# Shift and scale of both streams in a one-layer hybrid trunk: eight weight units in one run of requests, and one unsplit product in four column parts of the array

## The chip, the cores and the metric

The kernel runs on one core of a Trainium2 chip. The metric is device time in microseconds (us) of one execution, on all-float32 data. Lower is better.

## What is computed

One layer of a trunk over a latent stream (256 tokens) and a context stream (256 tokens), 1024 wide. Cut to what the change touches:

```
silu_c, silu_cc = silu(c), silu(c_ctx)                      # one vector for each stream
sh1_l, sc1_l, g1_l, sh2_l, sc2_l, g2_l = split(silu_c @ w_ada + b_ada, 6)
sh1_c, sc1_c, ...                      = split(silu_cc @ w_ada + b_ada, 6)
pl = (xl * (1 + sc1_l) + sh1_l) @ w_in                      # latent
pc = (xc * (1 + sc1_c) + sh1_c) @ w_in                      # context
... four token mixers on pl, pc, output projection, norm ...
... 32 experts (top 4), w_gate, w_up, w_down: 1024 x 1024 each, norm ...
```

`w_ada` is 1024 x 6144. Its first two sections of 1024 columns (shift and scale, sections 0 and 1) are needed for both streams before the input projection can start. The other four are needed later and for the latent stream alone.

## The kernel before

**Stages.** A front (projections and token mixers, until about 370 us) and then a loop over 32 experts whose weights (402.7 MB in float32) stream through a ring of buffers. The front is six generators (`gdn`, `within`, `side`, `ada_late`, `prep`, `dense`) that a written string, `ORDER`, weaves step by step (`weave`): each letter runs one step of one generator. So every engine gets its instructions in a fixed order, and each engine works through its own in that order. SP issues nearly all loads (`load`, L266), also in a fixed order: a load whose buffer is not free holds up all loads behind it. The loads are counted on eight semaphores in turn, so a load also waits until the load eight places before it has landed.

**Weight units.** The weights of the front come in units of 1 MB (2 of the 8 row blocks of `w_ada` by 1024 columns), named by section and part: ada(0,0) to ada(0,3), ada(1,0) to ada(1,3). There are four buffers, "spots" (`ring` tags r0 to r3). `issue(spot)` asks for the next unit of that spot's queue and `done(key)` calls it when a unit has been read. Spots 0 to 3 first hold ada(0,h), then ada(1,h). Behind these, spots 0 and 1 take the projection weights `uB`, `uK`, `uV` and so on in turn, and spot 2 takes the later sections: ada(2,0) is its third unit. `beside` hangs other loads on a unit: the input `xT` in two halves behind ada(1,3) and behind the first half of `uB`.

**Shift and scale** (`ada_first`, L416 on, and `ada_tail`). For each unit two row blocks k are multiplied. The even one is split into a rounded part and a rest (ACT L434 and DVE L435, in buffer `adap`) and multiplied by the split vectors `s4` (4 columns: two streams, two parts) in four fast products of 512 columns (L438). The odd one is multiplied unsplit, as float32, in two products (L429). `ada_tail` copies the sums (4 rows) out of PSUM, turns them with 8 small transposes (L455) and adds the bias on DVE into `mod`.

**What follows.** `prep` makes the operands: for each k of product B it modulates the input (`modulate`, ACT L543, DVE L544 and L545) and splits the weight slice (`split`, ACT L552 and DVE L553). `dense` runs the products of B for each k: 12 matmuls of 432 columns (L557 to L559), then K, V and the rest. `ada_late` multiplies the units of the later sections by the vector on ACT (L643) and sums them on POOL (L645, L647). ACT's order has the first of these, on ada(2,0), between the operands of k = 2 and k = 3 of product B.

Of the kernel before, what the change touches and what calls it, by code (L numbers as in the profile page):

```python
# [11 lines left out]
F32 = mybir.dt.float32  # L12
# [11 lines left out]
D = 1024  # L24
# [174 lines left out]
def trunk(ctx: ExitStack, tc: tile.TileContext, I, out, offs, dbg=None, nexp=NE):  # L199
# [82 lines left out]
    pa, pb = (held.tile([128, 4096], F32, tag=f"pair{i}", name=f"before{i}") for i in range(2))  # L282
    va = pb[:, 0:width(oa)]
    load(va[:, 0:64], I['va'][:, 0:64])

    def A(k):
        o, n = oa[k]
# [30 lines left out]
    queues[0] += prods[0::2]  # L318
# [4 lines left out]
    def issue(spot):  # L323

        if not queues[spot]:
            return
        key = queues[spot].pop(0)
        u = ring.tile([128, 2048], F32, tag=f"r{spot}", name="u" + "_".join(str(x) for x in key))
        if key[0] == 'ada':
            _, sec, h = key  # L330
            u = u.rearrange("p (k f) -> p k f", k=2)
            load(u, w_ada[:, 2 * h:2 * h + 2, sec * D:(sec + 1) * D])
        elif key[0] == 'out':
            u = u.rearrange("p (k f) -> p k f", k=2)
            load(u, w_out[:, 2 * key[1]:2 * key[1] + 2])
        else:
            c, h = key
            width_ = sum(b - a for a, b in COLS[c])
            n = 8 if c in 'KV' else 4
            u = u[:, 0:n * width_].rearrange("p (k f) -> p k f", k=n)  # L340
            o = 0
            for a, b in COLS[c]:
                load(u[:, :, o:o + b - a], w_in[:, n * h:n * h + n, a:b])
                o += b - a
        for dst, src in beside.pop(key, []):
            load(dst, src)
        open_units[key], spot_of[key] = u, spot

    def take(key):
# [1 line left out]

    def done(key):

        issue(spot_of[key])

    for spot in range(4):
        issue(spot)


    places = {}  # L360
# [49 lines left out]
    s4 = cst.tile([128, 8, 4], F32R, name="s4")  # L410
    sT3 = sT.rearrange("p (k v) -> p k v", v=2)
    S_.activation(s4[:, :, 0:2], sT3, AF.Copy)
    V.tensor_sub(s4[:, :, 2:4], sT3, s4[:, :, 0:2])


    def ada_first():  # L416

        tails = []
        for sec in range(2):
            ps = [(bank, fbank)[sec](f"psada{sec}{n}") for n in range(2)]  # L420
            for h in range(4):
                if sec == 1:
                    next(tails[0], None)
                u = take(('ada', sec, h))
                for kk in range(2):
                    k = 2 * h + kk
                    if kk:
                        for n in range(2):
                            P_.matmul(ps[n][0:2], sT3[:, k], u[:, kk, n * 512:(n + 1) * 512], start=False, stop=(k == 7), skip_group_check=True)  # L429
                        done(('ada', sec, h))  # L430
                    else:
                        w2 = early([128, 2, D], F32R, (0, 1, 3)[(4 * sec + h) % 3], f"adap{sec}{k}")
                        hi, lo = w2[:, 0], w2[:, 1]
                        S_.activation(hi, u[:, kk], AF.Copy)  # L434
                        V.tensor_sub(lo, u[:, kk], hi)  # L435
                        for w in (hi, lo):
                            for n in range(2):
                                P_.matmul(ps[n][0:4], s4[:, k], w[:, n * 512:(n + 1) * 512], start=(k == 0 and w is hi), stop=False, skip_group_check=True)  # L438
                    yield
            tails.append(ada_tail(sec, ps))  # L440
        yield from tails.pop()
        have.add('mod')

    def ada_tail(sec, ps):

        r4 = fp.tile([128, D], F32, tag="kTn", name=f"r4{sec}")[0:4]
        for n in range(2):
            if sec and n:
                V.tensor_copy(r4[:, n * 512:(n + 1) * 512], ps[n][0:4])
            else:  # L450
                S_.activation(r4[:, n * 512:(n + 1) * 512], ps[n][0:4], AF.Copy)
# [5 lines left out]
        p4 = pt[:, 0:32].rearrange("p (c v) -> p c v", v=4)  # L457
        V.tensor_tensor(mod[:, sec], p4[:, :, 0:2], bada[:, 8 * sec:8 * sec + 8].unsqueeze(2).to_broadcast([128, 8, 2]), op=OP.add)
        V.tensor_tensor(mod[:, sec], mod[:, sec], p4[:, :, 2:4], op=OP.add)
        if sec == 1:  # L460
            V.tensor_single_scalar(mod[:, sec], mod[:, sec], 1.0, op=OP.add)

# [235 lines left out]
        V.scalar_tensor_tensor(dst, u, 3.0, less, op0=OP.subtract, op1=OP.mult)  # L698


    mst = early(list(I["masks"].shape), I32, 3, "mst")
    load(mst, I['masks'])
# [1402 lines left out]
```

## Time and profile before

| what | value |
|---|---|
| device time, three runs | 1442.87, 1443.89, 1446.61 us (median 1443.89) |
| profiled execution: its time, its span | 1443.94 us, 1442.0 us |
| PE / DVE / ACT / POOL busy | 80% / 34% / 21% / 13% of the span |
| bytes moved by DMA | 460.59 MB, mean 319 GB/s |
| section 0 and 1 of `w_ada`: first request, `mod` complete | 1.15 us, 46.6 us |
| first expert product | about 386 us |

The shares are averages over the front and the experts. The change lies in the first 60 us, so that stretch is to be read: when each load is asked for and lands, which engine waits for it, and what in that stretch the rest of the front hangs on.

### The profile page before, as it was taken

The page shows a single profiled execution, that of the slowest core. Times are in us where ns is not written, and L with a number is a line of the kernel's source. Part 1 is how long each engine was busy: PE and PEld are TensorE (multiplying, and loading weights), DVE is VectorE, ACT ScalarE, POOL GpSimd, SP SyncE. Part 2 cuts the span into 40 slices and gives each one's busy share as a digit, 9 for nine tenths or more (in the row PEclk, how much of TensorE's full clock was granted, in tenths as well). Part 3 has the DMA queues.
Part 4 walks back from the last instruction along what each step waited for, and adds up shares of the span by engine and source line. Part 5 has one row for each costly group of instructions (what it writes and reads, how often), then busy time and mean ns, then how long its engine had stood idle before and what let it go on. Part 6 is the DMA issues. An engine that isn't in the chain of part 4 may idle for free.

```text
span 1442.0 us, 26141 instructions
## 1 busy us (share of the span) xinstructions
PE 1150.8 (80%) x11226; PEld 708.8 (49%) x11226; DVE 489.6 (34%) x863; ACT 297.6 (21%) x576; POOL 192.5 (13%) x229
## 2 busy tenths in 40 slices
PE   6797999899697897787787988686677869767783
PEld 1576888678444544354333643353333434433342
DVE  3767767979511211212022211121121112211116
ACT  3456644444210111111010101010001001101012
POOL 0242243450200100010000100010000101000002
PEclk9998979999698998998797989898879989898997
DMA  7634334418796998999943999999999999999970
GB/s 286 239 110 131 111 117 148 175 67 317 317 419 262 417 420 357 418 416 417 385 159 129 412 419 418 417 418 416 419 412 419 408 408 420 405 417 418 416 287 30
DMA packets 129059, 460.59 MB, mean 319 GB/s; under 512 B 9488, under 2 KB 19088, under 8 KB 128048
## 3 DMA queue, kind: packets, MB, share of 16 engines
q1 hardware_dynamic: 128816, 457.52, 79.8%
q8 instruction: 131, 2.15, 0.6%
q14 instruction: 112, 0.92, 0.2%
HBM read 456.45 MB, written 1.05 MB: 317 GB/s over the span
## 4 chain that ended last, share of the span: by engine, by line
PE 54%; DMA 22%; DVE 11%; issue 8%; ACT 4%; SPq 1%; DVEq 0%; ACTq 0%
PE g L1768 18%; PE four L1768 11%; DMA ring<-in_w_down 11%; DMA ring<-in_w_up 6%; PE xb L1750 6%; PE four L1814 3%; DMA ring<-in_w_gate 2%; PE fb L1786 2%; DMA bd<-in_b_down 1%; DMA uada<-in_w_ada 1%; PE psada L429 1%; DVE gt L1794 1%; PE psW L1005 1%; ACT scr L1796 1%; SPq L266 1%
## 5 line engine op out<-in xcount | busy, mean ns | idle before, releaser
L1768 PE MATMUL g<-ring,X 128*32 128x256 f32 (+1 forms) x3680 | 355.9, 472 | 142.2 <-issue 87.5
L1768 PEld LDWEIGHTS g<-ring,X 128*32 128x32 f32 (+1 forms) x3680 | 157.2, 128 | 320.2 <-issue 233.8
L1768 PE MATMUL four<-ring,X 128*32 128x256 f32 (+1 forms) x2272 | 208.6, 435 | 20.3 <-DMA ring<-in_w_down 19.6
L1824 DVE SCALAR_TENSOR_TENSOR rows<-four,cw,rows 128x1024 f32<-128x1024 f32 x66 | 81.7, 1280 | 329.6 <-PE four L1814 329.6
L1794 DVE TENSOR_TENSOR gt<-fb,vc 128x256 f32<-128x256 f32 (+1 forms) x37 | 18.7, 504 | 423.7 <-PE fb L1786 423.7
L1768 PEld LDWEIGHTS four<-ring,X 128*32 128x32 f32 (+1 forms) x2272 | 86.0, 118 | 123.5 <-issue 60.9
L1750 PE MATMUL xb<-Sg,hl 128*128 128x96 f32 x1024 | 135.4, 288 | 4.5 <-DVE Sg L1736 2.6
L1750 PEld LDWEIGHTS xb<-Sg,hl 128*128 128x128 f32 x1024 | 125.6, 200 | 27.2 <-issue 24.6
L1736 POOL TENSOR_SCALAR Sq<-slots,rank 128x128 f32<-128x128 f32 x62 | 39.4, 647 | 580.8 <-PE xb L1758 342.2
L1772 ACT ACTIVATE sA<-g 128x256 f32<-128x256 f32 (+1 forms) x33 | 14.0, 423 | 342.5 <-PE g L1768 342.5
L645 POOL TENSOR_TENSOR adas<-adas,uada 128x1024 f32<-128x1024 f32 x24 | 59.8, 2492 | 99.3 <-ACT uada L643 98.9
L1736 POOL TENSOR_SCALAR Sg<-slots,rank 128x96 f32<-128x96 f32 x62 | 31.6, 521 | 301.1 <-PE xb L1750 257.3
L1752 ACT ACTIVATE X<-xb 128x384 f32<-128x384 f32 x64 | 31.4, 491 | 123.4 <-PE xb L1750 117.9
L1796 ACT ACTIVATE scr<-gt 128x256 f32<-128x256 f32 (+1 forms) x37 | 17.7, 480 | 172.8 <-DVE gt L1795 172.8
L1772 ACT ACTIVATE sA<-four 128x256 f32<-128x256 f32 (+1 forms) x30 | 12.8, 427 | 163.1 <-PE four L1768 163.1
L1814 PE MATMUL four<-sA,ST 32*128 32x256 f32 (+1 forms) x512 | 42.7, 406 | 1.6 <-DVE sA L1985 1.6
L643 ACT ACTIVATE uada<-uada,sT 128x1024 f32<-128x1024 f32 x32 | 35.7, 1140 | 9.4 <-DMA uada<-in_w_ada 9.2
L1802 DVE TENSOR_TENSOR X<-fb,vc 128x256 f32<-128x256 f32 (+1 forms) x36 | 18.0, 499 | 54.2 <-PE fb L1786 54.2
L1005 PEld LDWEIGHTS <-before 64*64 64x64 f16 x1088 | 29.8, 115 | 9.8 <-issue 3.8
L1814 PEld LDWEIGHTS four<-sA,ST 32*128 32x128 f32 (+1 forms) x512 | 28.1, 188 | 6.5 <-DVE sA L1985 2.1
L1797 DVE TENSOR_TENSOR gt<-gt,scr 128x256 f32<-128x256 f32 (+1 forms) x37 | 18.9, 510 | 20.5 <-ACT scr L1796 20.5
L1768 PE MATMUL four<-ring,Xm 128*64 128x512 f32 x96 | 21.1, 592 | 0.0
(560 smaller groups left out, 1558.0 us busy)
## 6 DMA issues: line engine op xcount, KB each, us to landing
ring<-in_w_gate SPq DMA_DIRECT2D x128, 1024.0 KB, 18.1
ring<-in_w_up SPq DMA_DIRECT2D x128, 1024.0 KB, 17.8
ring<-in_w_down SPq DMA_DIRECT2D x128, 1024.0 KB, 18.1
uada<-in_w_ada SPq DMA_DIRECT2D x24, 1024.0 KB, 5.3
uout<-in_w_out SPq DMA_DIRECT2D x4, 1024.0 KB, 5.2
uE<-in_w_in SPq DMA_DIRECT2D x2, 1024.0 KB, 5.5
uF<-in_w_in SPq DMA_DIRECT2D x4, 512.0 KB, 4.0
uG<-in_w_in SPq DMA_DIRECT2D x2, 1024.0 KB, 5.3
```

The costliest lines, as they stand in the source:

```text
L643: S_.activation(u[:, kk], u[:, kk], AF.Copy, scale=sT3[:, 2 * h + kk, 0:1])
L645: G_.tensor_tensor(acc_, acc_, u[:, kk], op=OP.add)
L1005: P_.matmul(ps[cs, x * 64:x * 64 + 64], L[cs, x], R[cs, x] if len(R.shape) == 3 else R[cs], start=True, stop=True, skip_group_check=True)
L1736: eng.tensor_scalar(Sm[:, t, 0:m * n].rearrange("p (q s) -> p q s", s=n), slots[:, a:a + n].unsqueeze(1).to_broadcast([128, m, n]), rank[: ...
L1750: P_.matmul(xb[:, o:o + n], hl[:, t, k * 128:(k + 1) * 128], Sm[:, t, 0:n], start=(k == ks[0] and t == 0), stop=(t == 1), skip_group_check ...
L1752: S_.activation(X[:, ks[0] * n:(ks[-1] + 1) * n], xb[:, 0:len(ks) * n], AF.Copy)
L1768: P_.matmul(ps[n * q:n * q + n, 0:m], x(k), w[:, kk * 1024 + q * m:kk * 1024 + (q + 1) * m], start=(k == 0), stop=(k == 7), skip_group_che ...
L1786: P_.transpose(fb[:, c * 128:(c + 1) * 128], s[:, c * 128:(c + 1) * 128], ident)
L1794: V.tensor_tensor(g, p, bias(Cv('bg'), e, n), op=OP.add)
L1796: S_.activation(sg, g, AF.Sigmoid, scale=1.702)
L1814: P_.matmul(four[:, b, t * 256:(t + 1) * 256], st_[n * q:n * q + n, t * 128:(t + 1) * 128], Y[n * q:n * q + n, i * 256:(i + 1) * 256], sta ...
L1824: V.scalar_tensor_tensor(a, ps[t], cw[:, t, e:e + 1], a, op0=OP.mult, op1=OP.add)
```

## The change

Three things change.

1. **Loads.** The four units of section 1 no longer wait for the spots of section 0. They get buffers of their own (`extra`: three ring buffers that the split had used or that are filled later, and the upper half of `pa`). SP asks for them right behind section 0, then for both halves of the input and the masks, and only then for anything that hangs on `done`. Spot 0 and 1 go on to `uB` and spot 2 to ada(2,0) as soon as the products of section 0 have read them.
2. **Products.** Nothing is split. The vectors stand in a zeroed array `s32` with 32 columns for each row block. Each unit takes four float32 products of 512 columns, one for each row block and column half, and each goes to its own 32 output rows (columns of the array): 32 products in all in place of 48.
3. **Tail.** One PSUM bank (128 rows) is copied out by ACT, turned in four 128 x 128 transposes, and DVE adds the bias and the two row-block parts with strided views.

```diff
+    extra = [early([128, 2048], F32, i, f"uada1{i}") for i in (0, 1, 3)] + [pa[:, 2048:4096]]
-    beside['ada', 1, 3] = [(xus[0], xT[0])]
-    beside['B', 0] = [(xus[1], xT[1])]
-    first_ada = [('ada', sec, h) for sec in range(2) for h in range(4)]
+    first_ada = [('ada', 0, h) for h in range(4)]
...
     for spot in range(4):
         issue(spot)
+    for h in range(4):
+        load(take(('ada', 1, h)), w_ada[:, 2 * h:2 * h + 2, D:2 * D])
+    mst = pb[:, 2048:2048 + I["masks"].shape[1]].bitcast(I32)
+    for dst, src in ((xus[0], xT[0]), (xus[1], xT[1]), (mst, I['masks'])):
+        load(dst, src)
...
+    s32 = pb[:, 3200:3456].rearrange("p (k v) -> p k v", v=32)
+    V.memset(s32, 0.0)
+    V.tensor_copy(s32[:, :, 0:2], sT3)
...
                 for kk in range(2):
-                    k = 2 * h + kk
-                    if kk:
-                        for n in range(2):
-                            P_.matmul(ps[n][0:2], sT3[:, k], u[:, kk, n * 512:(n + 1) * 512], start=False, stop=(k == 7), skip_group_check=True)
-                        done(('ada', sec, h))
-                    else:
-                        w2 = early([128, 2, D], F32R, (0, 1, 3)[(4 * sec + h) % 3], f"adap{sec}{k}")
-                        hi, lo = w2[:, 0], w2[:, 1]
-                        S_.activation(hi, u[:, kk], AF.Copy)
-                        V.tensor_sub(lo, u[:, kk], hi)
-                        for w in (hi, lo):
-                            for n in range(2):
-                                P_.matmul(ps[n][0:4], s4[:, k], w[:, n * 512:(n + 1) * 512], start=(k == 0 and w is hi), stop=False, skip_group_check=True)
-                    yield
+                    for n in range(2):
+                        q = 2 * kk + n
+                        P_.matmul(ps[32 * q:32 * q + 32], s32[:, 2 * h + kk], u[:, kk, n * 512:(n + 1) * 512], start=(h == 0), stop=(h == 3), skip_group_check=True)
+                done(('ada', sec, h))
+                yield
...
-        for c in range(8):
-            P_.transpose(pt[:, 4 * c:4 * c + 4], r4[:, c * 128:(c + 1) * 128], ident[0:4, 0:4])
+        for c in range(4):
+            P_.transpose(pt[:, 128 * c:128 * c + 128], r[:, c * 128:(c + 1) * 128], ident)
```

SP's order of loads (output tile, input, shape; in brackets what the issue waits for: a DMAHW is one of the eight semaphores of earlier loads, an engine's name is work of that engine), from the last unit of section 0 on. Before:

```order
L266 DMA cons_89<-in_cons 128x640
L266 DMA mst<-in_masks 128x1152
L266 DMA uada_0_150<-in_w_ada 128x2x1024 [waits DMAHW0_49,DMAHW1_49,DVE_49,PE_49]
L266 DMA uada_1_185<-in_w_ada 128x2x1024 [waits DMAHW3_49,DVE_49,PE_49]
L266 DMA uada_2_196<-in_w_ada 128x2x1024 [waits DMAHW2_49,DMAHW4_49,DVE_49,PE_49]
L266 DMA uada_3_207<-in_w_ada 128x2x1024 [waits DMAHW5_49,DVE_49,PE_49]
L266 DMA xu_92<-in_xT 128x2048
L266 DMA uB_224<-in_w_in 128x4x384 [waits DMAHW0_49,DVE_49,PE_49]
```

The same place after (`uada_87` to `uada_89` and the first `before_84` are section 1; `before_84` from `in_xT` is the second half of the input):

```order
L266 DMA cons_92<-in_cons 128x640
L266 DMA uada_87<-in_w_ada 128x2x1024
L266 DMA uada_88<-in_w_ada 128x2x1024 [waits DMAHW0_49]
L266 DMA uada_89<-in_w_ada 128x2x1024 [waits DMAHW1_49]
L266 DMA before_84<-in_w_ada 128x2x1024 [waits DMAHW2_49]
L266 DMA xu_95<-in_xT 128x2048 [waits DMAHW3_49]
L266 DMA before_84<-in_xT 128x2048 [waits DMAHW4_49]
L266 DMA before_85<-in_masks 128x1152 [waits DMAHW5_49]
L266 DMA uB_151<-in_w_in 128x4x384 [waits DMAHW6_49,PE_49]
```

Section 1 and the input now wait for earlier loads alone and no longer for DVE and PE; behind the masks the order of `uB`, `vb`, `cons` and ada(2,0) is as it was.

PE's order for section 1. Before, its second and third unit:

```order
L438 MATMUL psada_210<-adap_238,s_110 4x512 [waits Activation_49]
L438 MATMUL psada_211<-adap_238,s_110 4x512
L438 MATMUL psada_210<-adap_238,s_110 4x512 [waits DVE_49]
L438 MATMUL psada_211<-adap_238,s_110 4x512
L429 MATMUL psada_210<-uada_1_185,sT 2x512 [waits DMAHW1_49]
L429 MATMUL psada_211<-uada_1_185,sT 2x512
```

After, its second to fourth unit and the transposes of its tail:

```order
L438 MATMUL psada_199<-uada_88,before_85 32x512 [waits DMAHW0_49]
L438 MATMUL psada_199<-uada_88,before_85 32x512 x3
L438 MATMUL psada_199<-uada_89,before_85 32x512 [waits DMAHW1_49]
L438 MATMUL psada_199<-uada_89,before_85 32x512 x3
L438 MATMUL psada_199<-before_84,before_85 32x512 [waits DMAHW2_49]
L438 MATMUL psada_199<-before_84,before_85 32x512 x3
L452 MATMUL psadT_235<-cons_92,r_233 128x128 [waits DVE_49,Activation_49]
L452 MATMUL psadT_235<-cons_92,r_233 128x128 x3
```

PE now waits for the load of each unit alone; the waits for ACT and DVE inside a unit are gone, and everything behind the tail stands as before.

## Rows read from the trace of the kernel before

**Rows 1.** Page part 2: 40 equal slices, DMA busy tenths and GB/s
```profile
DMA  7634334418796998999943999999999999999970
GB/s 286 239 110 131 111 117 148 175 67 317 317 419 262 417 420 357 418 416 417 385 159 129 412 419 418 417 418 416 419 412 419 408 408 420 405 417 418 416 287 30
```

**Rows 2.** Chain that ended last, in time order: start us, us, what; 45 to 61
```profile
45.05 9.44 DMA uada<-in_w_ada
...
55.57 1.13 ACT uada L643
57.23 2.16 DVE xu L544
60.54 0.60 DVE hlB L553
```

**Rows 3.** Timeline of SP's issues: start us, us, engine line op out<-in xcount
```profile
14.75 16.04 SPq L266 DMA_DIRECT2D uada<-in_w_ada  x4
30.84 0.46 SPq L266 DMA_DIRECT2D xu<-in_xT  x1
...
45.05 14.58 SPq L266 DMA_DIRECT2D uada<-in_w_ada  x2
```

**Rows 4.** Timeline of ACT and PE, 46 to 59 us, idle before in brackets
```profile
46.61 0.60 ACT L543 ACTIVATE xl<-xu,mod 128x256 fp32r<-128x256 f32 x1 [2.07 <-DVE mod L461]
...
47.61 0.55 ACT L552 ACTIVATE hlB<-uB 128x432 fp32r<-128x432 f32 x1
...
54.51 2.19 ACT L643 ACTIVATE uada<-uada,sT 128x1024 f32<-128x1024 f32 x2 [3.48 <-DMA uada<-in_w_ada]
...
58.96 0.36 PE L557 MATMUL pB<-hlB,xl 128*128 128x432 f32 x1
```

**Rows 5.** DMA issues at 4.26, 30.84 and 45.05 us: KB, us to landing
```profile
cons<-in_cons SPq DMA_DIRECT2D x1, 320.0 KB, 12.1
...
xu<-in_xT SPq DMA_DIRECT2D x1, 1024.0 KB, 7.6
...
uada<-in_w_ada SPq DMA_DIRECT2D x1, 1024.0 KB, 9.4
```

**Rows 6.** Stretches: us, busy (instructions) by engine, PEclk, DMA share, GB/s
```profile
10.00:15.00 5.00, 5.00 (x9) 0.80 (x9) 3.35 (x7) 1.47 (x2) 0.00 (x0) 1.00 1.02 418
35.00:40.00 5.00, 5.00 (x22) 1.34 (x20) 3.46 (x9) 1.06 (x1) 0.00 (x0) 1.00 1.01 363
...
41.00:42.00 1.00, 1.00 (x4) 0.10 (x3) 0.29 (x1) 0.00 (x0) 0.00 (x0) 1.00 0.79 263
```

**Rows 7.** Timeline of PE and ACT: products, PSUM copy and transposes
```profile
21.13 3.57 PE L429 MATMUL psada<-uada,sT 128*2 128x512 f32 x4
25.69 1.88 PE L429 MATMUL psada<-uada,sT 128*2 128x512 f32 x4
...
29.57 0.59 ACT L451 ACTIVATE r<-psada 4x512 f32<-4x512 f32 x1 [7.65 <-PE psada L429]
...
230.42 0.63 PE L1017 MATMUL pskwT<-cons,kw 128*128 128x128 f32 x4 [0.98 <-DVE kw L1070]
...
398.47 3.66 PE L1768 MATMUL four<-ring,X 128*32 128x256 f32 x64
```

**Rows 8.** Product B at both clocks (timeline), and two stretches as in rows 6
```profile
50.01 0.56 PE L557 MATMUL pB<-hlB,xl 128*128 128x432 f32 x1
50.37 0.56 PE L558 MATMUL pB<-hlB,xl 128*128 128x432 f32 x1
...
58.76 0.36 PE L559 MATMUL pB<-hlB,xc 128*128 128x432 f32 x1
...
100.00:120.00 20.00, 19.22 (x169) 17.98 (x167) 17.18 (x37) 14.79 (x27) 4.79 (x2) 1.00 0.33 101
...
182.00:199.00 17.00, 17.00 (x164) 15.06 (x164) 7.67 (x14) 6.99 (x12) 4.39 (x2) 0.50 0.27 88
```

More of the change, by code (lines that the diff above doesn't have):

```diff
@@ L346, in issue @@
             load(dst, src)
+        if key[0:2] == ('ada', 0):
+            h = key[2]
+            open_units['ada', 1, h], spot_of['ada', 1, h] = extra[h].rearrange("p (k f) -> p k f", k=2), None
         open_units[key], spot_of[key] = u, spot
@@ L352, in done @@
     def done(key):
-        issue(spot_of[key])
+        if spot_of[key] is not None:
+            issue(spot_of[key])
     for spot in range(4):
         issue(spot)
+    for h in range(4):
[3 more added lines that the diff above has]
+        load(dst, src)
     places = {}
@@ L409, in trunk @@
     V.tensor_copy(bada, A('b_ada'))
-    s4 = cst.tile([128, 8, 4], F32R, name="s4")
     sT3 = sT.rearrange("p (k v) -> p k v", v=2)
-    S_.activation(s4[:, :, 0:2], sT3, AF.Copy)
-    V.tensor_sub(s4[:, :, 2:4], sT3, s4[:, :, 0:2])
+    s32 = pb[:, 3200:3456].rearrange("p (k v) -> p k v", v=32)
+    V.memset(s32, 0.0)
+    V.tensor_copy(s32[:, :, 0:2], sT3)
     def ada_first():
@@ L419, in ada_first @@
         for sec in range(2):
-            ps = [(bank, fbank)[sec](f"psada{sec}{n}") for n in range(2)]
+            ps = (bank, fbank)[sec](f"psada{sec}")
             for h in range(4):
@@ L424, in ada_first @@
                 u = take(('ada', sec, h))
+                yield
                 for kk in range(2):
-                    k = 2 * h + kk
-                    if kk:
-                        for n in range(2):
-                            P_.matmul(ps[n][0:2], sT3[:, k], u[:, kk, n * 512:(n + 1) * 512], start=False, stop=(k == 7), skip_group_check=True)
-                        done(('ada', sec, h))
-                    else:
-                        w2 = early([128, 2, D], F32R, (0, 1, 3)[(4 * sec + h) % 3], f"adap{sec}{k}")
-                        hi, lo = w2[:, 0], w2[:, 1]
-                        S_.activation(hi, u[:, kk], AF.Copy)
-                        V.tensor_sub(lo, u[:, kk], hi)
-                        for w in (hi, lo):
-                            for n in range(2):
-                                P_.matmul(ps[n][0:4], s4[:, k], w[:, n * 512:(n + 1) * 512], start=(k == 0 and w is hi), stop=False, skip_group_check=True)
-                    yield
+                    for n in range(2):
+                        q = 2 * kk + n
+                        P_.matmul(ps[32 * q:32 * q + 32], s32[:, 2 * h + kk], u[:, kk, n * 512:(n + 1) * 512], start=(h == 0), stop=(h == 3), skip_group_check=True)
+                done(('ada', sec, h))
+                yield
             tails.append(ada_tail(sec, ps))
@@ L444, in ada_tail @@
     def ada_tail(sec, ps):
[L446 to L451, printed above, removed]
+        r = t512(f"r{sec}")
+        S_.activation(r, ps, AF.Copy)
         yield
         pt = xbank(f"psadT{sec}")
-        for c in range(8):
-            P_.transpose(pt[:, 4 * c:4 * c + 4], r4[:, c * 128:(c + 1) * 128], ident[0:4, 0:4])
+        for c in range(4):
+            P_.transpose(pt[:, 128 * c:128 * c + 128], r[:, c * 128:(c + 1) * 128], ident)
         yield
-        p4 = pt[:, 0:32].rearrange("p (c v) -> p c v", v=4)
-        V.tensor_tensor(mod[:, sec], p4[:, :, 0:2], bada[:, 8 * sec:8 * sec + 8].unsqueeze(2).to_broadcast([128, 8, 2]), op=OP.add)
-        V.tensor_tensor(mod[:, sec], mod[:, sec], p4[:, :, 2:4], op=OP.add)
+        p4 = pt.rearrange("p (c k n v) -> p k n c v", c=4, k=2, n=2)[:, :, :, :, 0:2]
+        m = mod[:, sec].rearrange("p (n c) v -> p n c v", n=2)
+        b = bada[:, 8 * sec:8 * sec + 8].rearrange("p (n c) -> p n c", n=2).unsqueeze(3).to_broadcast([128, 2, 4, 2])
+        V.tensor_tensor(m, p4[:, 0], b, op=OP.add)
+        V.tensor_tensor(m, m, p4[:, 1], op=OP.add)
         if sec == 1:
@@ L698, in rsqrt2 @@
         V.scalar_tensor_tensor(dst, u, 3.0, less, op0=OP.subtract, op1=OP.mult)
-    mst = early(list(I["masks"].shape), I32, 3, "mst")
-    load(mst, I['masks'])
     G_.tensor_copy(masks, mst)
```

## The prediction

> **What bounds the kernel now.** First the page's slices [rows 1]: the DMA engines are nearly full in the expert loop, but in the first third of the span they are half idle. There the engines' own order and waits set the time, and whatever the front loses early, the experts start later. I found nothing in the chain behind about 60 us that is tied to absolute time: up to the experts it runs through DVE, ACT and PE work that follows from product B on. So the change is worth what it takes off the start of that work.
>
> What starts it is not where one looks first. `mod` is complete just before 46.61, when ACT stops waiting for it [rows 4], and the first weight slice of B is split at 47.61. But the chain of waits does not pass there. It passes through the load of ada(2,0), asked for at 45.05, then ACT's L643 on it, DVE's modulation of k = 3 and the slice behind that [rows 2]. ACT stood 3.48 us before L643 for this load, until 54.51 [rows 4]; since ACT works in order, the operands of k = 3 wait for a load that has nothing to do with product B. PE has the products of k = 0 to 2 to do meanwhile and begins k = 3 at 58.96. So **the clock to watch is the landing of ada(2,0), T: 54.5 us before** (45.05 + 9.4 [rows 5]).
>
> T is late because the loads stop and go. Section 1 is asked for over 16 us from 14.75 on, since each spot must first be read by ACT, DVE and PE; the input follows at 30.84 [rows 3]. All of `uB`, `vb`, `cons` and ada(2,0) stand behind them on SP.
>
> **The change part by part: the loads.** In the new order SP never waits for ACT or DVE before `uB`, and for PE only where section 0 has long been read. What stays is the wait for the load eight places earlier. Six to eight loads, several MB, are then outstanding, so I take the queue to be full from the first request to ada(2,0). Its landings, step by step:
>
> - `cons2`, the last load before section 1, lands at 4.26 + 12.1 = 16.4 as before [rows 5]; nothing ahead of it moves.
> - Then section 1 (4 x 1.049 MB), the input (2 x 1.049) and the masks (0.590): 6.88 MB. A full queue moved 418 GB/s [rows 6]. 16.5 us, so masks land at 32.9; on the way the last unit of section 1 at 26.4 and the two input halves at 29.0 and 31.5.
> - Then `uB` twice (0.885 each), `vb` (0.189), `cons` (0.819), ada(2,0) (1.049): 3.83 MB, 9.2 us at the full rate. The trace shows more. From the landing of the input's first half, 30.84 + 7.6 = 38.4 [rows 5], to T = 54.5 passed 16.1 us with these loads and the input's second half (2.5 us) in it: 13.6 us. The rates in it sag [rows 6]: `uB` has rows of 128 and 64 bytes, and at 41 to 42 us the engines were 79% busy. For lack of backlog I take off 0.5 us, an estimate (0.2 of it is that row): 13.1. The bounds are 9.2 and 13.6, and I stand at the upper one because these are the same loads.
>
> T = 32.9 + 13.1 = **46.0**, against 54.5: **8.5 us earlier**; by the bounds 42.1 to 46.5.
>
> **The products.** They must only not be later than this. A unit's four float32 products go to four column parts. In the expert loop such products run side by side: 64 of 256 columns in 3.66 us, 57 ns each, so four of 512 columns take 0.46 us, or 0.92 at half the clock [rows 7]. A unit arrives every 2.5 us. The last lands at 26.4; then products (0.9), the copy out of PSUM (0.6 [rows 7]), four transposes (0.6 [rows 7], up to 1.3 at half clock), three small DVE steps and five hand-overs, about 1.2: `mod` at 29.7 to 30.4. The input is there at 29.0. The first `uB` lands at about 36 (masks 32.9, then 2.1 to 4 us). So product B starts at about 36 and not at 46.6, `mod` has 6 us of slack, and the eight splits on ACT and DVE are removed from a place where they no longer count: nothing for them in the sum. If that cover were gone, a late `mod` would cost us for us.
>
> **Where the stall goes.** B's start gains some 10 us, but ACT again meets L643 after three slices, at about 36 + 4.4 = 40.4 (46.61 to 54.51 - 3.48 before [rows 4]), and waits there until 46.0, longer than before. From T on, everything stands in the same order with the same durations, so the rest of the front and the experts move by the 8.5 us. Queued behind the new waits are `uB` and all later loads of SP; they are in the sum. The masks' conversion on POOL comes after 33 us instead of early; who reads it comes after product B. The copy of B's sums out of PSUM now also waits for the masks, landed some 20 us before. The `memset` of `s32` and its copy lie before the first unit has landed.
>
> **Sum.** Profiled execution 1443.94 us (span 1442.0 and 1.94 around it; the median of the runs is 1443.89, the same) - 8.5 = **1435.4 us**.
>
> **The rivals.**
>
> *The queue is slower than I read it.* In 35 to 40 us, fully busy, it moved 363 GB/s [rows 6]. With that rate from 16.4 on, the masks land 2.5 us later: T = 48.5, 1437.9 us. The Trainium skill (DMA: Bandwidth & Descriptors, Specifications) puts a core's share of HBM at about 358 GB/s; by it, as an estimate, the time would be 1438.1. The trace disagrees with its 418 over five us. Chance 0.07.
>
> *The queue is not kept full.* Eight semaphores in turn bound what is outstanding; if the small pieces of `uB` hold their turn, or landings come in bursts, SP stops again. With half of the old stop-and-go, T = 50: 1439.4. This is the case in which the change doesn't do what it says. Chance 0.04.
>
> *The four products of a unit don't run side by side.* One after the other at half clock a unit takes 3.6 us (3.57 for four [rows 7]), longer than its load. The first unit of section 1 lands at 18.9; with a backlog of two units of section 0 by then (an estimate: three small filter layers stand ahead of them in PE's order), six units end at 40.5, `mod` comes at 43.6, L643 after three slices at 48: 1437.4. At the full clock (1.88 [rows 7]) it hides. The expert loop's row speaks against it. Chance 0.04, inside the forecast's range.
>
> *The clock falls elsewhere.* Stretches in which PE is busy without a pause and yet has half the clock exist: 17 us from 182 on, 17.00 busy, granted clock 0.50 [rows 8]. At the full clock that work takes half, so such a stretch costs 8.5 us, as much as the whole gain. The front's pattern moves with the change, and one more may appear (1443.9, no change, chance 0.09), or this one may go (1426.9, chance 0.06).
>
> *Slower: PE stays at half clock in product B and K.* In the new opening PE does some 0.5 to 0.9 us of work in 2.5 us and then pauses from `mod` to the landing of `uB`; it starts B at 1.2 GHz. The trace shows what that is: B's matmuls start 0.36 us apart at 50.01 and 0.20 at 58.76, on 2.4 GHz [rows 4, 8]; before, the low level had ended by then, under steady work. The Trainium skill (TensorE: Matmul & The Clock Gate, The HAM clock gate) states it as a rule: half clock is the default and activity releases it. By it alone the opening's thinner PE work is a loss; the trace agrees that PE slows after waits, and shows also that it recovers. If it recovers as before, nothing is lost: 36 products of k = 0 to 2 take 13 us from 36 even at 1.2 GHz, done at 49, while k = 3 comes at 46.0 + 4.5 = 50.5. If the low level holds through all of B it costs at most 96 x 0.16 = 15 us, part of which hides behind B's earlier start and its waits for ACT and DVE, and through K, where PE is nearly saturated at the full clock (19.22 of 20 us [rows 8]), some 10 more. Of these 25 I take 15: 1450. It turns to a loss once it costs more than 8.5, so past B. Against it: B's own recovery above. Chance 0.04.
>
> **How the numbers follow.** The forecast has 0.66, with T from 42.1 to 47 (1431.5 to 1436.5) and a spread of some 2 us, as the runs of the kernel before show it. The range leaves out the extra half-clock stretch, the vanished one and the loss (0.09 + 0.06 + 0.04) and reaches over the slow and the starved queue: 1429 to 1441 us. A measurement can tell about 0.3% from no change, 4.3 us here, so 1439.6 is the bound of faster: forecast 0.66, serial products 0.04, vanished stretch 0.06, most of the slow queue 0.05 and half of the starved one 0.02 make 0.83. No change: the extra stretch 0.09 and the rest of the two queue cases 0.04, 0.13. Slower: 0.04.
>
> **What would show it.** Right: loads without a gap from 2 to about 46 us at over 400 GB/s until the masks; ACT waits for `uB` near 36 and not for `mod`; it then waits for ada(2,0) at L643 until about 46; the first expert product comes 8 to 9 us earlier. Wrong in a step: T outside 42 to 48; PE still in section 1 after 28 us; the first expert product moved by another amount than T, which would put the difference into the front's clock.

## The result, and the profile after

The changed kernel takes 1465.95 us (median of 4 runs, 1465.62 to 1468.86) beside 1444.01 for the kernel before on the same chip (4 runs, 1442.87 to 1446.61): a ratio of 1.0154, 95% interval 1.0135 to 1.0173. It is slower by some 22 us; forecast were 8.5 us less. The profiled execution has a span of 1464.0 us against 1442.0.

The front of the kernel did what was forecast. Timeline of PE and ACT of the changed kernel up to the landing of ada(2,0): start us, us, engine line, operation, count, in brackets the idle time before it and what ended it.

```profile
24.51 1.06 PE L438 MATMUL psada<-uada,before 128*32 128x512 f32 x8 [0.53 <-DMA uada<-in_w_ada]
27.06 1.93 PE L438 MATMUL psada<-before,before 128*32 128x512 f32 x8 [1.48 <-DMA before<-in_w_ada]
...
31.48 0.60 ACT L542 ACTIVATE xl<-xu,mod 128x256 fp32r<-128x256 f32 x1 [1.83 <-DVE mod L460]
...
36.22 0.56 ACT L551 ACTIVATE hlB<-uB 128x432 fp32r<-128x432 f32 x1 [3.65 <-DMA uB<-in_w_in]
...
45.01 1.15 ACT L642 ACTIVATE uada<-uada,sT 128x1024 f32<-128x1024 f32 x1 [5.35 <-DMA uada<-in_w_ada]
```

The products of the last two units wait for their loads, `mod` is complete at 31.5 us, the first slice of `uB` comes at 36.2 and ada(2,0) at 45.0. The last of these is the row that answers to L643 at 54.51 in [rows 4]: **T moved from 54.5 to 45.0**. The kernel also entered the experts early. The load with which the chain of waits enters the expert loop, in the kernel before (start us, us, what):

```profile
374.45 11.09 DMA ring<-in_w_gate
```

and in the changed one:

```profile
359.70 11.57 DMA ring<-in_w_gate
```

The lead is 14.75 us: 9.5 from T, and the rest from the stretch that had half the clock before, the last of [rows 8] (6.8 us more there, 1.6 lost again before the experts). In the changed kernel its row (us, busy time and instructions of PE, PEld, DVE, ACT and POOL, granted clock, DMA share, GB/s) is

```profile
182.00:199.00 17.00, 16.34 (x322) 14.70 (x318) 15.08 (x20) 8.25 (x13) 12.03 (x37) 1.00 0.39 126
```

The granted clock is 1.00 in place of 0.50, that is 2.4 GHz in place of 1.2, and PE gets through 322 instructions there in place of 164 (not quite the same ones, since this kernel is 9.5 us ahead).

**So all that was lost was lost in the expert loop**, which no line of the change touches. From that load to the end of the span the kernel before took 1067.5 us, the changed one 1104.3: 36.8 us more. Two things differ there. The first stands in the page's slices of the changed kernel (tenths of the clock and of the DMA engines' time, GB/s), which answer to [rows 1]:

```profile
PEclk8898999987898999797897999898979989898897
DMA  9633343449997989999724999999999999999970
GB/s 368 207 100 125 121 146 116 153 175 352 354 385 309 407 326 370 385 408 405 278 116 184 408 408 409 406 406 407 408 398 408 396 397 410 398 407 402 408 294 29
```

The DMA engines are as full as before, and where the kernel before moved 416 to 420 GB/s this one moves 406 to 410. One stretch of the loop, in the columns of the window row above, in the kernel before:

```profile
860.00:940.00 80.00, 62.18 (x411) 29.90 (x408) 14.08 (x23) 8.57 (x18) 4.79 (x9) 0.91 1.03 418
```

and in the changed one:

```profile
860.00:940.00 80.00, 60.73 (x321) 26.91 (x321) 15.12 (x22) 7.47 (x14) 4.41 (x8) 0.90 1.03 408
```

The second is on TensorE. The page's row of the queue that brings its instructions (packets, MB, share), before:

```profile
q8 instruction: 131, 2.15, 0.6%
```

and after:

```profile
q8 instruction: 140, 2.29, 0.7%
```

The waits of PE from 340 to 1440 us that nothing in the profile ended (us in total, times, longest), before:

```profile
PE g L1768 <- issue: 87.5, 17, 10.0
```

and after:

```profile
PE g L1765 <- issue: 127.3, 34, 10.4
```

There are 9 more instruction transfers, and twice as many waits "issue" ahead of or inside an expert's first products.

### The profile page after: what moved, and what is told of

The parts are those of the page before. It is cut to its first block, busy times and chain, and to the rows that moved or that the text cites. A ratio compares the mean times of both kernels' runs of the same rounds, so it can differ in the third digit from the quotient of the medians.

```text
span 1464.0 us, 26092 instructions
## 1 busy us (share of the span) xinstructions
PE 1139.0 (78%) x11218; PEld 707.1 (48%) x11218; DVE 483.1 (33%) x855; ACT 288.6 (20%) x566; POOL 192.9 (13%) x229
## 3 DMA queue, kind: packets, MB, share of 16 engines
q1 hardware_dynamic: 128816, 457.52, 80.3%
## 4 chain that ended last, share of the span: by engine, by line
PE 53%; DMA 22%; DVE 10%; issue 10%; ACT 4%; SPq 1%; DVEq 0%; ACTq 0%
PE g L1765 19%; DMA ring<-in_w_down 11%; PE four L1765 11%; PE xb L1747 6%; DMA ring<-in_w_up 5%; PE four L1811 2%; DMA ring<-in_w_gate 2%; PE fb L1783 2%; DMA before<-in_w_ada 1%; DMA bd<-in_b_down 1%; DMA uada<-in_w_ada 1%; DVE gt L1791 1%; PE psW L1002 1%; SPq L266 1%; ACT scr L1793 1%
## 5 line engine op out<-in xcount | busy, mean ns | idle before, releaser
L1765 PE MATMUL g<-ring,X 128*32 128x256 f32 (+1 forms) x3680 | 365.1, 477 | 171.9 <-issue 127.3
L1765 PE MATMUL four<-ring,X 128*32 128x256 f32 (+1 forms) x2272 | 205.2, 429 | 15.0 <-DMA ring<-in_w_down 14.1
L1821 DVE SCALAR_TENSOR_TENSOR rows<-four,cw,rows 128x1024 f32<-128x1024 f32 x66 | 81.7, 1279 | 326.6 <-PE four L1811 326.6
L1002 PEld LDWEIGHTS <-before 64*64 64x64 f16 x1088 | 29.7, 114 | 9.9 <-issue 4.1
L1783 PE MATMUL fb<-cons,sB 128*128 128x128 f32 x76 | 15.7, 303 | 7.5 <-ACT sB L1769 7.5
```

What stands on the lines that cost most here:

```text
L1002: P_.matmul(ps[cs, x * 64:x * 64 + 64], L[cs, x], R[cs, x] if len(R.shape) == 3 else R[cs], start=True, stop=True, skip_group_check=True)
L1765: P_.matmul(ps[n * q:n * q + n, 0:m], x(k), w[:, kk * 1024 + q * m:kk * 1024 + (q + 1) * m], start=(k == 0), stop=(k == 7), skip_group_che ...
L1783: P_.transpose(fb[:, c * 128:(c + 1) * 128], s[:, c * 128:(c + 1) * 128], ident)
L1821: V.scalar_tensor_tensor(a, ps[t], cw[:, t, e:e + 1], a, op0=OP.mult, op1=OP.add)
```

## The experiments

Two theories, one for each of these differences.

- **A, the buffers' place.** The change drops the tile `s4`, 128 bytes in each partition. Everything laid out behind it moved down by 128: by the built programs the experts' buffers start at a multiple of 256 bytes before and 128 past one after. The loads into them are slower for that.
- **B, TensorE's code.** The built program has 149,657 instructions of 64 bytes for TensorE before and 149,643 after, since products and waits of the opening are gone. Every block of the experts lies 14 instructions earlier. An instruction transfer is 16.4 KB (2.15 MB in 131), so its ends fall on other instructions, and at some experts TensorE runs out.
- **The rival to both**: the earlier entry, or another clock or phase, made the loop slower.

One table serves all runs: when DVE adds an expert's product into `rows` (L1821 in the changed kernel), at eight places of the loop. The first row has the times of the kernel before in us, the others the difference to it, each from the profiled execution. A number that stays the same along a row means that nothing is lost or won between. One execution is not the median: the profiled one of e1 is its shortest, 6 us under its median, and that of e4 is 9.5 us over it.

```
kernel before            405.3  497.3  634.4  678.6  769.9 1003.2 1259.2 1395.0
changed kernel           -14.7   -7.9   -2.3   -2.4   +6.4  +12.5  +15.6  +20.7
e1  gap                  -14.8   -9.6   -3.4   -3.5   +1.5   +1.8   +0.2   -0.3
e2  before, gap           -5.7   -5.9   -2.8   -1.6   +0.2   +6.6   +9.8  +15.1
e3  products, gap         -7.7   -2.3   +3.8   +3.7   +8.7   +9.2   +7.5   +8.9
e4  loads                 +2.1   +2.4   +2.7   +6.1   +5.9   +6.3   +6.2   +6.1
e5  gap, code            -15.2  -14.9  -12.3  -14.1  -12.5  -12.0  -11.9  -12.0
e6  before, code          +1.1   +6.5  +12.6  +12.4  +17.5  +18.6  +16.4  +17.8
e7  code                 -10.9  -11.0  -10.7   -4.2   -4.3   +5.5   +6.5  +12.8
e8  gap 64, code         -16.4  -15.2  -13.2   -9.5   -7.2   -0.7   +2.7  +10.7
e9  products, gap, code  -12.6  -12.7  -12.9   -9.6   -9.7   -9.5   -9.6   -8.3
e10 gap, code +64        -16.3  -15.5  -16.8  -15.9  -20.0  -19.2  -18.7  -19.6
e11 gap, code +128       -10.9   -7.9  -10.0   -7.4  -14.0  -13.4  -14.5  -18.3
e12 before, code +64      -4.5   -3.7   -4.9   -4.0   -8.2   -8.2   -6.9   -9.9
```

("gap": buffers where they stood before, except in e2, where a gap moves them off. "code": the experts' instructions where they lay before, except in e6, where they lie as in the changed kernel, and in e10 to e12, where they lie 64 or 128 instructions further than before.)

**e1, the buffers put back.** The changed kernel with one unused tile:

```
     V.tensor_copy(bada, A('b_ada'))
+    gap = cst.tile([128, 32], F32, name="gap")
     sT3 = sT.rearrange("p (k v) -> p k v", v=2)
```

> The changed kernel with one unused tile of 32 floats (128 bytes per partition) where the tile s4 stood. Its front reached the experts 14.8 us earlier than before, and the loss came behind that, with the expert loads at about 408 instead of 418 GB/s. Theory A (address): without s4 every buffer behind it starts 128 bytes lower, the weight buffers at 128 past a multiple of 256 instead of on one, and the loads are slower for that. Then the rate is back at 418 GB/s and the time is 1444 - 14.8 = 1429 us (1426 to 1432). Theory B (the change itself: more outstanding loads, another order of the ring's buffers, another phase of the clock in the experts): the tile changes nothing and the time stays at 1464 to 1468 us at 408 GB/s.

Measured: 1450.29 us (7 runs, before 1443.63), ratio 1.0059 (1.0035 to 1.0082). The rate is back, in the stretch shown above:

```profile
860.00:940.00 80.00, 61.58 (x408) 29.11 (x406) 13.41 (x22) 7.75 (x15) 4.39 (x8) 0.89 1.02 418
```

and from 770 us on the lag against the kernel before no longer grows. The buffers' place is a cause, as A says, but by the medians it gives back only 16 of the 37 us that the loop lost, and the 1426 to 1432 us of A alone were missed: before 770 us the lead of 14.8 us is lost all the same, in three jumps (the table's columns 497, 634 and 770). The chain of waits of this kernel at the first jump (start us, us, what) gave theory B:

```profile
462.79 1.02 PE g L1766 x11
463.82 4.19 issue
468.00 6.87 PE g L1766 x73
474.88 17.75 DMA ring<-in_w_down
```

After 11 products of the fourth expert TensorE stops for 4.19 us, and the profile shows nothing that it waits for. The weights then come late as well, because their places in the ring come free late. The trace's packet records have one instruction transfer in this gap, from 465.68 to 466.70 us, and one in each of the other eight stops of this kind in the loop of this run; in the changed kernel's nine it is the same.

**e2, the buffers of the kernel before moved off.** The same line added to the kernel before, which puts its buffers 128 bytes past a multiple of 256.

> The kernel before with the same unused 128 bytes added, so that its weight buffers start 128 past a multiple of 256. Theory A: the front is as before (experts from 374.5 us), the loads of the experts fall to about 408 GB/s and the time is 1444 + 37 = 1481 us (1470 to 1485). Theory B: 1444 us at 418 GB/s.

Measured: 1462.9 us (4 runs), ratio 1.0155 (1.0116 to 1.0193), and 408 GB/s in the stretch. A tile that nothing reads costs 19 us, not the 37 that I expected if A were the whole loss. The early jumps of e1 (columns 497, 634 and 770) are not there; most of what is lost is lost behind 770 us, some of it in steps (5 us at the addition at 972 us, 8 at 1283). This is what A alone looks like.

**e3, the products alone**: the changed kernel's products and tail with the loads asked for as before, and the gap.

```
-    for h in range(4):
-        load(take(('ada', 1, h)), w_ada[:, 2 * h:2 * h + 2, D:2 * D])
...
-    first_ada = [('ada', 0, h) for h in range(4)]
+    first_ada = [('ada', sec, h) for sec in range(2) for h in range(4)]
```

> The unsplit products, the new tail and the masks in the shared buffer alone; the weight units of section 1 and the input are asked for as in the kernel before, and the unused 128 bytes keep the old addresses. If the gain of the front comes from the loads alone, a unit here is still asked for only after the unit before it in its spot was read, but the read is faster, since no split stands ahead of it: the load of ada(2,0) lands perhaps 4 to 8 us earlier than before, and the time is 1444 less that, 1436 to 1440 us. If the products carried nothing, 1444.

Measured: 1456.5 us (4 runs), ratio 1.0103 (1.0068 to 1.0139). T came down to 47.7 us and the experts started 7 us early, but the time is 16 us over the range that I gave: the same three jumps as in e1 follow, at other times. Timeline of PE at the fourth expert:

```profile
469.91 1.02 PE L1761 MATMUL g<-ring,X 128*32 128x256 f32 x11 [0.69 <-DMA ring<-in_w_down]
475.32 3.21 PE L1761 MATMUL g<-ring,X 128*32 128x256 f32 x28 [4.39 <-issue]
```

TensorE stops after the same eleventh product, 7 us later in absolute time. It is tied to the instruction and not to the time, which speaks against the rival.

**e4, the loads alone**: the changed kernel's loads, with the split products as before (their buffers taken from a free pool).

```
-                        w2 = early([128, 2, D], F32R, (0, 1, 3)[(4 * sec + h) % 3], f"adap{sec}{k}")
+                        w2 = late.tile([128, 2, D], F32R, tag=f"l{h % 2}", name=f"adap{sec}{k}")
```

> The early requests alone: section 1, the input and the masks asked for as in the changed kernel, the products split as before, with the two buffers of the split where the modulated input stands later, and the old addresses. ACT and DVE need about 2.3 us for a split and PE 3 to 5 us for a unit, a little more than a load's 2.5 us. Theory of the prediction (the landing of ada(2,0) decides): that load lands at 45 to 46 us and the time is that of e1 within 3 us, about 1429 to 1434. If the products matter as well, mod comes so late that ACT reaches the stall at ada(2,0) after it has landed, and the time lies between, 1434 to 1440.

Measured: 1441.55 us (10 runs), ratio 1.0005 (0.9973 to 1.0038): no change, above both ranges that I gave, and no stop behind the fourth expert's eleventh product. (A step of 3 us at the column 679, which e9 has too and e7 with 6, I have not followed up.) ACT's timeline shows why the loads alone are worth little:

```profile
45.23 0.60 ACT L551 ACTIVATE xl<-xu,mod 128x256 fp32r<-128x256 f32 x1 [2.12 <-DVE mod L469]
...
49.57 1.14 ACT L651 ACTIVATE uada<-uada,sT 128x1024 f32<-128x1024 f32 x1
```

The load that set T is now there in time (no idle time stands before L651), and `mod` takes its place: with the splits it is complete only at 45.2, against 31.5 in the changed kernel. The work behind it is 3.6 us ahead at 181 us and 2.1 behind at the experts (the table's first column): from 164 to 232 us this execution had a granted clock of 0.80, the kernel before 0.87. It is also one of the three longest of the ten (1451 to 1456 us, the others 1437 to 1443), so its row in the table is not the usual one.

**e5, the code put back as well.** e1 with six small products ahead of the first one of the opening. They make TensorE's program 149,657 instructions long again, with every block of the experts where it lay before.

```
             ps = (bank, fbank)[sec](f"psada{sec}")
+            if sec == 0:
+                s16 = s32[:, 0, 2:18].bitcast(F16)
+                P_.matmul(ps[0:32, 0:16], s32[:, 0], A('c'), start=True, stop=True, skip_group_check=True)
+                for _ in range(5):
+                    P_.matmul(ps[0:32, 0:32], s16, s16, start=True, stop=True, skip_group_check=True)
```

> The changed kernel with the 128 bytes of the gap, so that its buffers stand where they stood before, and six small products ahead of the first one of the opening (one in float32, five in float16), written over by the first real product. They make TensorE's program as long as it was: the built program before has 149,657 instructions of 64 bytes there, the changed one 149,643 and this one 149,657, with every block of the experts at the same place as before. They run while TensorE waits for the first unit. Theory B, that the second loss comes from where TensorE's instructions lie, so that it runs out of them at the start of some experts: those waits go (before the lag jumped by 8 us at the fifth expert, 6 at the ninth and 5 at the eleventh), the 131 instruction transfers of queue 8 come back in place of 140, the lead of 14.8 us at the entry into the experts is kept to within the 4 to 6 us that the runs with the old program lost on the way: 1429 to 1435 us. The rival, that an earlier or another front meets the experts' loads in a worse phase, whatever the program: 1450 us as in e1, and the waits at the experts' starts stay.

Measured: **1432.43 us** (6 runs, 1430.95 to 1433.38, before 1443.23), ratio 0.9925 (0.9899 to 0.9950). The page has 131 instruction transfers. The waits from 340 to 1440 us:

```profile
PE g L1771 <- issue: 78.6, 16, 10.0
```

and PE's timeline at the fourth expert:

```profile
464.95 2.37 PE L1771 MATMUL g<-ring,X 128*32 128x256 f32 x40 [0.21 <-issue]
```

The nine transfers and the extra waits are gone, the fourth expert runs through its products, and of the 15 us of lead 12 are left at the table's last column, 11 at the end. Theory B holds: work that computes nothing, added in a pause of TensorE, made the kernel 18 us faster.

**e6, the code of the kernel before moved off**: 242 instructions (256 less 14) ahead of its first product, nothing else.

```
+            if sec == 0:
+                P_.matmul(ps[0][0:4, 0:16], s4[:, 0].bitcast(F32), A('c'), start=True, stop=True, skip_group_check=True)
+                for _ in range(119):
+                    P_.matmul(ps[0][0:4, 0:4], s4[:, 0], s4[:, 0], start=True, stop=True, skip_group_check=True)
```

> The kernel before with 242 more instructions on TensorE ahead of its first product (one float32 product and 119 of four columns, written over by the first real one), which puts every later instruction where the changed kernel has it, counted modulo 256 instructions (16 KB, the size of one instruction transfer): 242 is 256 less 14. Buffers stand as before. The products take some 8 to 15 us, in the time that TensorE waits for the first units. Theory B: about 1444 + 16 = 1460 us (1456 to 1463), waits of 3 to 4 us inside the first products of the fourth, eighth, tenth expert and so on, 140 instruction transfers and one more for the added code. The rival, that the program's place is nothing: 1444 us, and 131 or 132 transfers.

Measured: 1460.77 us (4 runs), ratio 1.0110 (1.0072 to 1.0148). The page has 141 instruction transfers, one of them for the added code. The waits as above:

```profile
PE g L1772 <- issue: 120.0, 34, 10.0
```

and PE's timeline at the fourth expert:

```profile
478.66 1.02 PE L1772 MATMUL g<-ring,X 128*32 128x256 f32 x11 [0.57 <-issue]
484.06 1.08 PE L1772 MATMUL g<-ring,X 128*32 128x256 f32 x8 [4.38 <-issue]
```

The stop is back behind the same eleventh product, in a kernel with the old front and the old loads, and the lag has the jumps of e1 and e3. Forward by 242 did what back by 14 had done, as it must if only the place within a transfer of 256 instructions counts.

**e7, the code alone put back**: e5 without the gap.

> The changed kernel with the same six small products, and no gap: its buffers stay 128 bytes past a multiple of 256. If the two causes are independent and add up, this run has the slow loads alone: 1429 + 20 = 1449 us (1446 to 1455) with 408 GB/s from 860 to 940 us; together with e1 (the loss of the program alone, 1450) it splits the 37 us that the experts lost. If the loss of the program was a consequence of the slow loads or the other way round: 1464 us as the changed kernel.

Measured: 1454.02 us (5 runs), ratio 1.0075 (1.0048 to 1.0103), at the slow rate:

```profile
860.00:940.00 80.00, 61.66 (x418) 31.15 (x422) 15.32 (x26) 8.46 (x18) 5.38 (x10) 0.89 1.03 407
```

With e1 and e5 this makes a table of four: neither put back 1.0154, buffers alone 1.0059, code alone 1.0075, both 0.9925. Each cause acts without the other, but they do not add up: alone they give back 0.0095 and 0.0079, together 0.0229. Part of that is the front, where e7's profiled execution had a granted clock of 0.87 from 164 to 232 us, against 1.00 in e1 and e5, and entered the experts 11 us early and not 15; the rest I leave open.

**e8, a gap of 64 bytes**: e5 with `[128, 16]` for the tile, buffers 192 past a multiple of 256.

> As e5 but with a gap of 64 bytes: every buffer of the experts starts 192 bytes past a multiple of 256. If the loads want a multiple of 256: 408 GB/s from 860 to 940 us or less, and some 1449 us, as e7. If only an odd multiple of 128 is slow: 418 GB/s and the time of e5. If the rate falls with the number of pieces that a row is cut into (two of unequal size here as there): 408 too.

Measured: 1452.58 us (8 runs), ratio 1.0062 (1.0040 to 1.0083):

```profile
860.00:940.00 80.00, 61.22 (x462) 31.04 (x458) 15.29 (x26) 8.69 (x18) 4.65 (x8) 0.91 1.03 407
```

Slow, like 128: of the three starts tried the multiple of 256 alone has the full rate.

**e9, the products alone with the code put back**: e3 with the six products of e5.

> The products alone, as in e3 (loads asked for as before, buffers where they stood before), with the six small products of e5, so that every block of the experts lies on TensorE where it lay before. If e3's loss in the experts, 16 us, came from the place of TensorE's instructions alone: the lead of 7.1 us that e3 had at the entry into the experts is kept to within 3 us, 1437 to 1440 us, and 131 instruction transfers. If the product change costs the experts something besides: nearer to the 1456 us of e3.

Measured: 1437.53 us (10 runs), ratio 0.9955 (0.9929 to 0.9982), 131 transfers. So the products are worth 6 us without the loads. Of the 21 us between the profiled executions of e3 and e9, 5 stand in the front (leads of 7.7 and 12.6 us at the experts, granted clocks of 0.87 and 0.97 from 164 to 232 us); the other 16 are what e3 loses more in the experts, with its other place of the code.

**e10 and e11, the code moved further**: e5 with 37 and 69 in place of 5 in the loop, so that the experts' blocks lie 64 and 128 instructions behind their old place.

> As e5 with 38 small products ahead in place of six: every later instruction of TensorE lies 64 instructions (4 KB) behind its place before. The front should be e5's within 1 us, since the products run while TensorE waits for the first unit. If the place decides only where the instruction transfers end within the experts' blocks, the time lies between that of e5 and that of e1, 1429 to 1452 us, with waits at other products than in either; if e5 gained by something that any delay or any warm-up of TensorE ahead of the first unit brings, e5's time, 1432 us.

> As e10 with 70 small products, 128 instructions (8 KB, half of one instruction transfer) behind the place before. The same two readings: between 1429 and 1452 us with waits at still other products, or e5's 1432 us whatever the place.

Measured: 1423.97 us (4 runs), ratio 0.9877 (0.9825 to 0.9928), and 1425.15 us (4 runs), ratio 0.9865 (0.9814 to 0.9917). Both lie below the span that I had written down for them, and both beat e5 by the medians; their intervals touch its interval. The old place was not the best one. In e10 the win is at the eleventh expert, the one with most rows. TensorE's wait there, before:

```profile
691.59 7.06 PE L1750 MATMUL xb<-SMm,hl 128*128 128x64 f32 x32 [13.10 <-issue]
```

and in e10:

```profile
670.79 7.06 PE L1753 MATMUL xb<-SMm,hl 128*128 128x64 f32 x32 [8.16 <-issue]
```

Yet e10 has more transfers (137) and more waits ahead of line g in all (106.9 us against 78.6 in e5). Their sum is no price: in e1 the stops at the tenth, fourteenth and eighteenth expert leave the lag within 1 us of where it was, the one at the fourth costs 8. I take it that a wait costs where the ring of loads is full and TensorE sets the end, not where the loads do; no run tests this.

**e12, that place in the kernel before**: 64 more instructions there (as e6, with 30 in place of 119).

> The kernel before with 64 more instructions on TensorE ahead of its first product (as e6, with 31 products), nothing else: the place of the experts' blocks that e10 has. If the 8 us between e5 and e10 are the place alone: 1444 - 8 = 1436 us (1433 to 1438), the lag against the kernel before falling by some 4 us at the eleventh expert and some 3 after the thirteenth, 137 instruction transfers. If the gain of e10 needed its own front: 1444 us.

Measured: 1435.07 us (10 runs, before 1441.72), ratio 0.9946 (0.9925 to 0.9966). The lag falls at the eleventh expert as in e10. Its wait there, in the list of PE's waits from 640 to 800 us:

```profile
PE xb L1754 <- issue: 8.3, 1, 8.3
```

So the same kernel with idle products ahead is 0.5% faster, with nothing of the change. Not all of it need be the place in the experts: of the 8.1 us at the end of the profiled execution 4.5 stood at the entry into them already, won from 182 to 199 us at a granted clock of 0.84 in place of 0.50, and some 4 came at the eleventh expert. How the median's 6.7 us divide is open. The 3 us expected behind the thirteenth expert did not last to the end. e10 is the fastest version by the median, e11 by the ratio: the change as it is, one unused tile, and some dozens of idle products, some 1.3% under the kernel before.

## Why the prediction was wrong

**The step that failed** is "From T on, everything stands in the same order with the same durations, so the rest of the front and the experts move by the 8.5 us". The order was the same. The durations were not: the change took away a tile and some instructions, and with them moved every buffer and every instruction that comes later. T moved by 9.5 us, and the expert loop took 36.8 us more. I searched the parts of the change for work and waits and costed `s4` and the removed products at nothing. None of the rivals was a loss in the expert loop; the only loss I gave was PE's clock in B and K, with 0.04.

Point by point, up to there:

- *The queue is full up to ada(2,0).* Right. The last unit of section 1 was used from 27.06 (landing forecast 26.4), `uB` came at 36.22 (36), T was 45.0 (46.0, bounds 42.1 to 46.5). From the masks' landing (33.4 against 32.9) to T passed 11.5 us, so the upper price for `uB`, `vb`, `cons` and ada(2,0), 13.1, was 1.6 us too high. The slow queue and the starved one did not happen.
- *The products don't hold up `mod`.* Right, but the term was half of what it should be: a float32 product is two PE instructions (a unit's four products are the x8 above), and I had read the 64 instructions of [rows 7] as 64 products. A unit took 1.06 us at the full clock and 1.93 at half of it, against 0.46 and 0.92; the price of the rival with serial products was halved in the same way. With loads every 2.5 us it still hides; `mod` came at 31.5 against 29.7 to 30.4.
- *The splits' removal counts nothing.* True of the sum, wrong as a reading of the change. With the loads alone (e4) `mod` came at 45.2 and took over as the last to arrive. With the products alone T fell to 47.7 (e3), I take it because the spots come free sooner. So at L643 the loads alone brought 4.9 us, the products alone 6.8, both 9.5: the sum gave to the loads what the products could nearly do without them.
- *ACT meets L643 early and waits.* Right: idle 5.35 us in place of 3.48 [rows 4].
- *The clock falls elsewhere.* The rival that the stretch from 182 on goes, which I gave 0.06, happened in the profiled execution: the lead grew from 9.5 to 16.3 us across it, 6.8 against the 8.5 that I gave it. From 164 to 232 us the granted clock was 0.80 to 0.87 in the kernel before, e3, e4, e6, e7 and e11, and 0.95 to 1.00 in the others, the kernel before with only a gap (e2) among these. So it is not the change that decides it, and some 5 us of any one profile here hang on it.
- *PE stays slow in B and K.* It did not: the granted clock, 0.50 from 36 to 40 us, was 0.94 from 40 to 45, and the lead was still 9.5 us at 171 us.

With the two side effects undone, e5 took 1432.43 us, 3 us under the forecast and inside its range. That it is so close is in part luck: its profiled execution was 10.3 us ahead at 181 us, won some 5 more where the clock was higher and lost 4 in the experts. The wait at ada(2,0) was the right one to price; what it was worth was hidden under two costs that the diff does not show.

## What to carry to other kernels

Compare the built programs before costing an edit: where the first byte of the big buffers lies, and how many instructions each engine's program has lost or gained. In this kernel an edit at the opening moved the experts by more than it won, and a few idle instructions and one unused tile undid it; measure an edit at two or three such places before judging it.

## What the runs showed of the hardware

**Where a load's rows start in SBUF.** Loads of 8 KB for each partition, from 860 to 940 us, into buffers that start at a multiple of 256 bytes: 417 to 419 GB/s. At 128 or 192 past one: 407 or 408 (before, e1, e5, e6 against after, e2, e7, e8). The packets are as many (128,816 on queue 1 in both), and one of 4,096 bytes takes 160 ns in that stretch at a multiple of 256 and 164 off one (trace records, the same runs). The Trainium skill (DMA: Bandwidth & Descriptors, How a descriptor splits into AXI transactions) says that a transfer off a multiple of 256 needs one more piece, and says it of reads; here only the address written to had moved. By its rule a packet of 4,096 bytes would be 17 pieces for 16, which as an estimate makes 393 GB/s from 418. The trace has 407 to 408, so here it costs less than half of that.

**TensorE's instructions are a load like others.** In the changed kernel, e1, e3 and e6, TensorE stops for 3.2 to 4.4 us inside the first products of an expert, behind product 11 of the fourth, 15 of the eighth, 17 of the tenth, 21 of the fourteenth, 25 of the eighteenth, and in the changed kernel and e1 each gap holds one instruction transfer of 16,384 bytes. The product's number is the expert's plus 7 each time, so the place of the stop moves evenly from expert to expert, as a boundary every 256 instructions would in equal blocks of code. In the kernel before, e2, e4, e5 and e7 to e12 none of these stops is there. The Trainium skill (Runtime: NRT & Kernel Launch, Instruction fetch mechanics) says that instructions come in blocks of 16 KiB, that passing from one to the next is mostly hidden, and that a branch taken out of the window makes the engine wait for its target. The traces agree with the block's size and with waits at the experts, whose code is chosen by branches. They differ on the first point: these stops come some products after an expert's start, and one cost 8 us in the end (in e1 the lead is 17.6 us at the third expert's addition into `rows` and 9.6 at the fourth's), while others cost nothing. Why behind just these products, and why 64 or 128 instructions further is better than the old place, stays open; no run took a branch away.
